# Low parts of weights on VectorE alone, half of the V product's chunks kept in PSUM over all groups, and the weight copies of gathered rows on ScalarE

## The chip, the core and the metric

The kernel runs on one core of one Trainium2 chip. A core has TensorE (PE, matrix products; the loading of a stationary operand is listed apart as PEld), VectorE (DVE), ScalarE (ACT), GpSimd (POOL) and SyncE (SP, which here only issues transfers). Each engine works through its own queue in order. SBUF holds the operands, and TensorE adds up its products in the eight banks of PSUM. The metric is the device time of one execution in microseconds (us).

## The reference, cut to what matters

The reference is a stack of transformer blocks on 512 tokens of width 1024, in float32. The part that the change touches most is the expert layer of the first block. Each token picks 128 of 16,384 experts (8 heads, 16 each) by two rounds of top-16 over products of queries with keys. An expert is one row of a table U and one row of a table V:

```
act = gelu(einsum('td,thkd->thk', x, u_tab[experts])) * gates
y   = einsum('thk,thkd->td', act, v_tab[experts])
```

The inputs are float32 and so is the result. The kernel therefore writes every matrix as a sum of a high and a low part and forms three products, high by high, high by low and low by high.

## The kernel before, in words

*Units and splits.* `weights` (L295) loads one unit of weights, 128 partitions by 1024, into one of the `w_raw` buffers (six in the expert layer). `split` (L284) makes its two parts. ScalarE copies `w_raw` to `w_hi` (L288). Then `w_lo = w_raw - w_hi` (L289) is made on VectorE, or on GpSimd where `eng=nc.gpsimd` is given. There are two buffers of `w_hi` and two of `w_lo`. `product` (L307) then runs 24 matrix instructions on the unit: first the 16 that use `w_hi`, last the 8 that use `w_lo`.

*The expert layer.* For the first 384 tokens ("dense" tokens) all experts are computed and weighted with gates that are mostly zero. For the last 128 tokens only the rows of their own experts are gathered, one token per partition. The layer goes through three stages here called retrieval, scatter and loop.

- Retrieval (`retrieve`): products with `wq`, scores against the keys, and the two rounds of top-16 on VectorE. Between them stand products of the dense tokens with units of U (`reach`, called through `ahead`), whose gelu is put away in DRAM.
- Scatter (`scatter_gates`): for each four tokens VectorE makes two one-hot tiles `hot` (L1216), GpSimd (L1217) and ScalarE (L1221) multiply one of them with the gates, and TensorE multiplies them to the table of gates. More `reach` products stand beside.
- Loop (in `peer`): 16 groups of 8 output chunks `m`. For each chunk VectorE multiplies a gelu tile with its gates (`f`, L949), it is split to `ga` (L288, L289), one unit of V is loaded and split, and one product of 24 instructions goes to a PSUM tile `mm`. VectorE then adds that to the running sum `h` (L984).

*The gathered rows.* `Own.go` (L1043) copies the number of a row to a tile `f` (or `gel`) on VectorE (L1053), and GpSimd issues an indirect transfer of that row of U or V to `own_row` (L1058). A row fetched earlier is used by `Own.use` (L1023): its weight is copied to the same tile `f` on VectorE (L1034), and one instruction of 128x1024 on VectorE multiplies it in (L1037 for U, L1041 for V). The copies tie the rows to the pace of the other work.

*Who makes the low part.* In retrieval, in scatter, in parts of the first block and in the `w_ab` products of the second block the low part is GpSimd's by argument. In the loop a small planner decides for each unit: `less_loaded` adds up costs (1.13 for a VectorE split, 2.3 for a GpSimd split, 1.2 and 1.04 for a row) and takes the engine that ends first. The order of instructions on each engine is made by a scheduler from its own estimate of times.

*PSUM.* In the expert layer four banks are `mm` and four are `aux`. In the loop only `mm` is used, until the end.

Of the kernel before, what the change touches and what calls it, by code (L numbers as in the profile page):

```python
# [11 lines left out]
F32 = mybir.dt.float32  # L12
# [44 lines left out]
def _pairs(b):  # L57
    """[32 groups, 64 states, 16 channels] -> block diagonal over pairs of groups [128, 16, 32]."""
# [15 lines left out]
def _half_cols(w):  # L74
    """The two members of every rotary pair into two halves of a head."""
# [110 lines left out]
class Ctx:  # L186
    """Pools and constants; tokens are `T` columns in `nb` PSUM banks of `hn` each."""
# [9 lines left out]
    def enter(self, name, side):  # L197
        """A pool that `leave` closes; once h is on the right, the sides are exchanged."""
# [13 lines left out]
    def psum(self, mm, aux):  # L212
        """PSUM as `mm` accumulators of all tokens and `aux` single banks."""
# [5 lines left out]
    def raw_units(self, n):  # L219
        """`n` buffers for units of weights, in an order that all that is loaded there keeps."""  # L220
# [5 lines left out]
    def work(self):  # L226
        """Pools of small tiles and of the tiles of norms."""
# [20 lines left out]
def newton_rsqrt(c, v, n):  # L248
    """1/sqrt(v) of a [128, n] tile, elementwise, to float32 accuracy."""
# [13 lines left out]
def exp_exact(c, out, x, n):  # L263
    """exp of a [128, n] tile to float32 accuracy."""
# [30 lines left out]
def weights(c, src, nk, n, eng=None):  # L295
    """Load one unit of weights and split it: two float32r views [128, nk, n]."""
# [5 lines left out]
    split(c, raw, hi, lo, eng=eng)  # L302
# [15 lines left out]
def token_stats(c, acc, width):  # L318
    """rsqrt(mean + eps) per token from partial sums acc [128, T]: [tokens of a tile, tiles]."""
# [15 lines left out]
def along_tokens(c, col):  # L335
    """A per-token column [128, tiles] as a row on all partitions: PSUM banks of `hn` tokens."""
# [15 lines left out]
def square_sum(c, acc, k, src, eng=None, scale=1.0):  # L352
    """acc += (src * scale) squared (the first chunk starts it)."""
# [9 lines left out]
def token_rows(c, acc, width, name):  # L363
    """rsqrt(mean + eps) as rows on all partitions, in SBUF, and as columns."""
# [4 lines left out]
def column_rows(c, col, name):  # L369
    """A per-token column as rows in SBUF."""  # L370
# [7 lines left out]
class Rows:  # L378
    """The rows of a norm, made when first asked for; uses of them wait until `hold` products are under way."""
# [20 lines left out]
class S5:  # L400
    """Powers of the discretised transition, the input and output weights of chunks of 4 tokens."""
# [74 lines left out]
    def scaled(self, dst, src, by, eng, name):  # L476
        """dst = src * by; parts along the second axis, `by` the real and the imaginary part and the negative of that."""
# [9 lines left out]
    def inputs(self, j):  # L487
        """The input weights of position j in a chunk; position 3 comes first."""
# [9 lines left out]
    def transposes(self):  # L498
        """The input weights as the stationary side of products."""
# [10 lines left out]
    def rotations(self, k):  # L510
        """The rotations of positions 2^k and more, after those before, of a chunk."""
# [11 lines left out]
    def powers(self):  # L523
        """The output weights of the state."""
# [17 lines left out]
    def inside(self, q):  # L542
        """The output weights of the chunk itself, of 4 pairs of groups."""
# [16 lines left out]
def s5_states(c, pool, xs, S, hf):  # L560
    """The states before each chunk, of 8 of the 16 pairs of groups; xs is [(position in chunk, channel), pair, chunk]."""
# [38 lines left out]
def s5_outputs(c, pool, xs, S, hf, h, ys):  # L600
    """ys = gelu of the outputs of these pairs."""
# [21 lines left out]
def mix_layer(c):  # L623
    """Block 1 up to the residual after w_out, which becomes c.h."""
    nc, d = c.nc, c.d
    tt = nc.vector.tensor_tensor
    with c.pool("mix", "right") as pool:
# [3 lines left out]
        with c.pool("s5", "right") as s5p:  # L631
# [3 lines left out]
            with c.pool("s5t", "right") as tmp:  # L635
                S = S5(c, s5p, outer, tmp)
                acc = c.norm("acc")
                for k in range(8):
                    x = pool.tile([128, 512], F32, name="u", bufs=5)
                    nc.sync.dma_start(x, d["xT"][:, k])  # L640
                    if k == 0:
                        w = weights(c, d["w_in"][0], 8, 128, eng=nc.gpsimd)
# [7 lines left out]
                for m in range(4):  # L650
                    ps = c.mm()
                    product(c, ps, [((w[0][:, k], w[1][:, k]), xk[k]) for k in range(8)])
                    if m < 3:
                        w = weights(c, d["w_in"][m + 1], 8, 128, eng=None if m else nc.gpsimd)
# [16 lines left out]
                for what, step in [(o[0], int(o[1])) for o in V_ORDER]:  # L671
                    if what == "v":
# [9 lines left out]
                        else:  # L682
                            w = weights(c, d["w_in"][4], 8, 128, eng=nc.gpsimd)
# [12 lines left out]
            for what, step in [(o[0], int(o[1])) for o in U_ORDER]:  # L696
                if what == "u":
                    ps = c.mm()
                    product(c, ps, [((w[0][:, k], w[1][:, k]), xk[k]) for k in range(8)])
                    if step < 3:  # L700
                        w = weights(c, d["w_in"][5 + step], 8, 128, eng=nc.gpsimd)
# [26 lines left out]
            def half(m, k0, pair):  # L728
                """Half of the product of output chunk m; weights come for two chunks at a time."""
# [60 lines left out]
def sgu_norm(c, vn, mean):  # L790
    """The norm of v [token, head, tile, channel] in place, from its sums over channels."""
# [14 lines left out]
def sgu_weights(c, pool):  # L806
    """The causal weights of the mixing, and what it adds."""
# [14 lines left out]
def sgu_mix(c, gp, u, vn, wb):  # L822
    """u *= causal mixing of the normalised v."""
# [21 lines left out]
PER_CALL = 0.6  # L845
# [6 lines left out]
PER_USE = 1.2  # L852
PER_FETCH = 1.04
W_POOL = 2.3
# [1402 lines left out]
```

## Time and profile before

| | |
|---|---|
| median of three runs | 3222.72 us (3222.37 to 3227.86) |
| span of the profiled execution | 3231.5 us |
| DVE busy | 2449.9 us, 76% |
| PE busy, PEld busy | 2989.7 us, 93%; 2704.9 us, 84% |
| ACT busy, POOL busy | 1269.3 us, 39%; 1261.8 us, 39% |

The profiled execution has its span as its only time. It is 0.3% longer than the median of the runs. The expert layer takes the stretch from 257 to 1657 us: retrieval to 598, scatter to 852, loop to 1657. Busy shares are means over stages with different limits, so each stage has to be read by itself. A wait row names the instruction that waited and the one that ended the wait.

### The profile page before, as it was taken

The page shows a single profiled execution, that of the slowest core. Times are in us where ns is not written, and L with a number is a line of the kernel's source. Part 1 is how long each engine was busy: PE and PEld are TensorE (multiplying, and loading weights), DVE is VectorE, ACT ScalarE, POOL GpSimd, SP SyncE. Part 2 cuts the span into 40 slices and gives each one's busy share as a digit, 9 for nine tenths or more (in the row PEclk, how much of TensorE's full clock was granted, in tenths as well). Part 3 has the DMA queues.
Part 4 walks back from the last instruction along what each step waited for, and adds up shares of the span by engine and source line. Part 5 has one row for each costly group of instructions (what it writes and reads, how often), then busy time and mean ns, then how long its engine had stood idle before and what let it go on. Part 6 is the DMA issues. An engine that isn't in the chain of part 4 may idle for free. (4 is left out here: it accounts for less than half of the span.)

```text
span 3231.5 us, 47250 instructions
## 1 busy us (share of the span) xinstructions
PE 2989.7 (93%) x17801; PEld 2704.9 (84%) x17801; DVE 2449.9 (76%) x4680; ACT 1269.3 (39%) x2170; POOL 1261.8 (39%) x786
## 2 busy tenths in 40 slices
PE   4878997899999999999999999899999999999999
PEld 3667997888999999899997899655999997778887
DVE  9977899999799999999998965664534446665352
ACT  3644332577633333333344433144323324443241
POOL 5335566787577677777754202011000012010000
PEclk8988998999999999999999999788999999999999
DMA  2213355566798899998952220011222221022232
GB/s 100 72 53 108 133 170 183 189 229 243 246 311 301 307 305 317 315 311 303 314 198 83 71 73 9 1 47 36 88 92 92 92 86 46 24 79 92 97 98 91
DMA packets 202888, 485.06 MB, mean 150 GB/s; under 512 B 25676, under 2 KB 95780, under 8 KB 199588
## 3 DMA queue, kind: packets, MB, share of 16 engines
q1 hardware_dynamic: 165796, 347.81, 32.3%
q0 software_dynamic: 36864, 134.23, 12.0%
q8 instruction: 140, 2.29, 0.3%
q14 instruction: 88, 0.72, 0.1%
HBM read 437.42 MB, written 44.55 MB: 149 GB/s over the span
## 5 line engine op out<-in xcount | busy, mean ns | idle before, releaser
L288 ACT ACTIVATE w_hi<-w_raw 128x1024 fp32r<-128x1024 f32 (+1 forms) x498 | 511.4, 1028 | 750.7 <-PE mm L314 627.2
L289 POOL TENSOR_TENSOR w_lo<-w_raw,w_hi 128x1024 fp32r<-128x1024 f32 x201 | 532.8, 2653 | 206.5 <-ACT w_hi L288 112.0
L289 DVE TENSOR_TENSOR w_lo<-w_raw,w_hi 128x1024 fp32r<-128x1024 f32 (+1 forms) x297 | 409.2, 1378 | 138.2 <-ACT w_hi L288 96.5
L314 PE MATMUL mm<-hn,w_hi 128*128 128x384 f32 (+1 forms) x2400 | 486.4, 351 | 1.8 <-DVE hn L289 1.3
L314 PEld LDWEIGHTS mm<-hn,w_hi 128*128 128x128 f32 x2400 | 429.0, 191 | 17.8 <-DVE hn L289 1.6
L314 PE MATMUL mm<-ga,w_hi 128*128 128x384 f32 x2048 | 389.6, 343 | 5.5 <-DVE ga L289 3.7
L314 PEld LDWEIGHTS mm<-ga,w_hi 128*128 128x128 f32 x2048 | 368.9, 193 | 8.0 <-DVE ga L289 5.1
L314 PE MATMUL mm<-xg,w_hi 128*128 128x264 f32 (+1 forms) x1920 | 345.9, 334 | 20.5 <-ACT w_hi L288 8.8
L360 POOL TENSOR_TENSOR acc<-acc,sq 128x512 f32<-128x512 f32 (+1 forms) x55 | 86.1, 1570 | 658.7 <-ACT sq L359 654.4
L314 PEld LDWEIGHTS mm<-xg,w_hi 128*128 128x128 f32 x1920 | 290.0, 191 | 59.2 <-DVE xg L292 12.4
L314 PE MATMUL mm<-hn,w_lo 128*128 128x384 f32 (+1 forms) x1200 | 259.1, 353 | 13.7 <-POOL w_lo L289 6.4
L314 PE MATMUL mm<-hid,w_hi 128*128 128x264 f32 (+1 forms) x1536 | 251.1, 319 | 0.0
L1058 POOL DMA_INDIRECT own_row<-V_rows,f x128 | 204.9, 1601 | 92.2 <-DVE f L1034 52.1
L314 PEld LDWEIGHTS mm<-hid,w_hi 128*128 128x128 f32 x1536 | 223.0, 188 | 20.0
L314 PEld LDWEIGHTS mm<-hn,w_lo 128*128 128x128 f32 x1200 | 214.8, 191 | 25.8 <-DVE w_lo L289 9.3
L314 PE MATMUL mm<-ga,w_lo 128*128 128x384 f32 x1024 | 207.3, 345 | 30.8 <-DVE w_lo L289 20.6
L288 ACT ACTIVATE ga<-f 128x384 fp32r<-128x384 f32 x128 | 67.0, 525 | 378.3 <-DVE f L949 370.9
L314 PEld LDWEIGHTS mm<-ga,w_lo 128*128 128x128 f32 x1024 | 182.5, 192 | 38.9 <-DVE w_lo L289 24.2
L1041 DVE SCALAR_TENSOR_TENSOR own_x<-own_row,f,own_x 128x1024 f32<-128x1024 f32 x123 | 195.6, 1590 | 0.5
L314 PE MATMUL mm<-xg,w_lo 128*128 128x264 f32 (+1 forms) x960 | 173.6, 329 | 0.0
L1058 POOL DMA_INDIRECT own_row<-U_rows,f x87 | 129.1, 1484 | 83.5 <-DVE f L1034 64.5
L314 PEld LDWEIGHTS mm<-xg,w_lo 128*128 128x128 f32 x960 | 144.9, 188 | 17.1
(732 smaller groups left out, 5357.2 us busy)
## 6 DMA issues: line engine op xcount, KB each, us to landing
w_raw<-U SPq DMA_DIRECT2D x128, 512.0 KB
w_raw<-V SPq DMA_DIRECT2D x128, 512.0 KB
w_raw<-w_f SPq DMA_DIRECT2D x128, 512.0 KB
g_all<-stage SPq DMA_DIRECT2D x24, 1024.0 KB
g<-g_all SPq DMA_DIRECT2D x32, 768.0 KB
early<-gel SPq DMA_DIRECT2D x70, 192.0 KB
gel<-early SPq DMA_DIRECT2D x70, 192.0 KB
w_raw<-w_ab SPq DMA_DIRECT2D x22, 512.0 KB
```

What stands on the lines that cost most here:

```text
L288: nc.scalar.activation(hi, src, AF.Copy)
L289: (eng or nc.vector).tensor_tensor(lo, src, hi.bitcast(F32), ALU.subtract)
L314: c.nc.tensor.matmul(ps[:, h, :hn], lhsT=st[a], rhs=mv[b][:, h * hn:(h + 1) * hn], start=first and i == 0, stop=last and i == len(order) - 1)
L360: (eng or nc.gpsimd).tensor_tensor(acc, acc, sq, ALU.add)
L1041: stt(self.acc, r, weight, self.acc, op0=ALU.mult, op1=ALU.add)
L1058: nc.gpsimd.indirect_dma_start(out=r, out_offset=None, in_=self.c.d["U_rows" if i0 < 128 else "V_rows"], in_offset=bass.IndirectOffsetOnAx ...
```

## The change

All low parts are made on VectorE: the argument `eng` and the planner `less_loaded` with its constants are gone. In the loop the products of chunks 0 to 3 (`HELD = 4`) go to four `aux` banks that keep adding up over all 16 groups. These are added to `h` once, in the last group. Chunks 4 to 7 are as before. The copy of a gathered row's weight is a ScalarE instruction. The final transposes of the gathered rows' sum (`add`) use an `mm` bank, as the `aux` banks are taken. The changed file has its comment strings blanked, and its line numbers are 3 to 9 lower from the loop on.

```diff
-def split(c, src, hi, lo, scale=None, eng=None):
+def split(c, src, hi, lo, scale=None):
     if scale is None:
         nc.scalar.activation(hi, src, AF.Copy)
-        (eng or nc.vector).tensor_tensor(lo, src, hi.bitcast(F32), ALU.subtract)
+        nc.vector.tensor_tensor(lo, src, hi.bitcast(F32), ALU.subtract)
...
-            w = weights(c, d["U"][a], 8, 128, eng=eng)
+            w = weights(c, d["U"][a], 8, 128)
...
-        def less_loaded():
-            k = 0 if load[0] + 1.13 <= load[1] + W_POOL else 1
-            load[k] += (1.13, W_POOL)[k]
-            return (nc.vector, nc.gpsimd)[k]
...
+            held = [c.aux()[:, None, :] for _ in range(HELD)]
...
-                    w = weights(c, d["V"][8 * g + m], 8, 128, eng=less_loaded())
-                    ps = c.mm()
-                    product(c, ps, [((w[0][:, k], w[1][:, k]), (ga[0][:, k], ga[1][:, k])) for k in range(8)], n=n)
+                    w = weights(c, d["V"][8 * g + m], 8, 128)
+                    keep = m < HELD
+                    ps = held[m] if keep else c.mm()
+                    product(c, ps, [((w[0][:, k], w[1][:, k]), (ga[0][:, k], ga[1][:, k])) for k in range(8)], n=n,
+                            first=not keep or g == 0, last=not keep or g == 15)
                     if g < 15:
                         pace(1)
-                    tt(c.h[m][:, :n], ps[:, 0, :n], c.h[m][:, :n], ALU.add)
+                    if not keep or g == 15:
+                        tt(c.h[m][:, :n], ps[:, 0, :n], c.h[m][:, :n], ALU.add)
...
         if at is not None:
-            nc.vector.tensor_copy(at, weight)
+            nc.scalar.activation(at, weight, AF.Copy)
             weight = at
...
-            w = weights(c, d["wq"][2 * h + k], 8, 128, eng=nc.gpsimd)
+            w = weights(c, d["wq"][2 * h + k], 8, 128)
...
-    load = lambda m: weights(c, d["w_ab"][m], 8, 128, eng=nc.gpsimd)
+    load = lambda m: weights(c, d["w_ab"][m], 8, 128)
```

The order of VectorE's queue in the loop, in the half where rows of V are used: before, one stretch reads as follows (`own_x` is the sum of the gathered rows, `ga` a low part of the activations, `h<-mm` the addition of a product).

```order
L1041 SCALAR_TENSOR_TENSOR own_x<-own_row,f,own_x 128x1024
L949 TENSOR_TENSOR f<-gel_11585,g 128x384
L1053 COPY f<-own_ids 128x1
L984 TENSOR_TENSOR h<-mm,h 128x384
L1034 COPY f<-own_gate 128x1
L289 TENSOR_TENSOR w_lo<-w_raw,w_hi 128x1024
L1041 SCALAR_TENSOR_TENSOR own_x<-own_row,f,own_x 128x1024
L289 TENSOR_TENSOR ga<-f,ga 128x384
L1041 SCALAR_TENSOR_TENSOR own_x<-own_row,f,own_x 128x1024
L984 TENSOR_TENSOR h<-mm,h 128x384
L289 TENSOR_TENSOR w_lo<-w_raw,w_hi 128x1024
```

Here half of the units' `w_lo` stand on this queue, and the others on GpSimd's. In the changed kernel a stretch of the same half of the loop reads:

```order
L1032 SCALAR_TENSOR_TENSOR own_x<-own_row,f,own_x 128x1024
L1044 COPY f<-own_ids 128x1
L975 TENSOR_TENSOR h<-mm,h 128x384
L289 TENSOR_TENSOR w_lo<-w_raw,w_hi 128x1024
L289 TENSOR_TENSOR ga<-f,ga 128x384
L1032 SCALAR_TENSOR_TENSOR own_x<-own_row,f,own_x 128x1024
L938 TENSOR_TENSOR f<-gel_10968,g 128x384
L975 TENSOR_TENSOR h<-mm,h 128x384
L289 TENSOR_TENSOR w_lo<-w_raw,w_hi 128x1024
L1044 COPY f<-own_ids 128x1
L1032 SCALAR_TENSOR_TENSOR own_x<-own_row,f,own_x 128x1024
```

The copies `f<-own_gate` are gone from the queue, the additions `h<-mm` come for half of the chunks only, and every unit's `w_lo` stands in it.

In retrieval VectorE's queue holds the top-16 instructions (MAX, MAX_INDEX and MATCH_REPLACE, which the profile calls MAX8, FIND_INDEX8 and MATCH_REPLACE8; `s`, `i` and `rep` are what they make for one half of a head). A stretch of it before:

```order
L1094 MAX s_2444<-rep_2551 128x8
L1094 MAX s_2444<-rep_2557 128x8
L1095 MAX_INDEX i_2445<-s_2444,rep_2551 128x8
L1095 MAX_INDEX i_2445<-s_2444,rep_2557 128x8
L1093 MATCH_REPLACE rep_2563<-s_2444,sc 128x128
L1093 MATCH_REPLACE rep_2569<-s_2444,sc 128x128
L1094 MAX s_2444<-rep_2563 128x8
L1094 MAX s_2444<-rep_2569 128x8
L1095 MAX_INDEX i_2445<-s_2444,rep_2563 128x8
L1095 MAX_INDEX i_2445<-s_2444,rep_2569 128x8
```

No split stands in it. The same instructions in the changed kernel:

```order
L1085 MAX s_2444<-rep_2551 128x8
L289 TENSOR_TENSOR w_lo<-w_raw,w_hi 128x1024
L1085 MAX s_2444<-rep_2557 128x8
L1086 MAX_INDEX i_2445<-s_2444,rep_2551 128x8
L1086 MAX_INDEX i_2445<-s_2444,rep_2557 128x8
L1084 MATCH_REPLACE rep_2563<-s_2444,sc 128x128
L1084 MATCH_REPLACE rep_2569<-s_2444,sc 128x128
L1085 MAX s_2444<-rep_2563 128x8
L1085 MAX s_2444<-rep_2569 128x8
L1086 MAX_INDEX i_2445<-s_2444,rep_2563 128x8
L1086 MAX_INDEX i_2445<-s_2444,rep_2569 128x8
```

Splits, which stood on GpSimd's queue, now stand among the top-16 instructions, and the instructions behind a split come after it.

ScalarE's queue in the loop, before:

```order
L288 ACTIVATE ga<-f 128x384
L288 ACTIVATE w_hi<-w_raw 128x1024
L288 ACTIVATE ga<-f 128x384
L288 ACTIVATE w_hi<-w_raw 128x1024
L288 ACTIVATE ga<-f 128x384
L288 ACTIVATE w_hi<-w_raw 128x1024 x2
L897 ACTIVATE gel<-mm 128x384
```

It holds copies to `ga` and `w_hi` and the gelu only. A stretch of it in the changed kernel:

```order
L288 ACTIVATE w_hi<-w_raw 128x1024
L1025 ACTIVATE f<-own_gate 128x1 x2
L288 ACTIVATE w_hi<-w_raw 128x1024
L894 ACTIVATE gel<-mm 128x384
L1025 ACTIVATE f<-own_gate 128x1 x3
L288 ACTIVATE ga<-f 128x384
L288 ACTIVATE w_hi<-w_raw 128x1024
L1025 ACTIVATE f<-own_gate 128x1
L288 ACTIVATE ga<-f 128x384
L288 ACTIVATE w_hi<-w_raw 128x1024
```

The copies `f<-own_gate` of 128x1 now stand between the copies that make the high parts.

## Rows read from the trace of the kernel before

**Rows 1.** The page's part 5, GpSimd's splits of all stages.

```profile
L289 POOL TENSOR_TENSOR w_lo<-w_raw,w_hi 128x1024 fp32r<-128x1024 f32 x201 | 532.8, 2653 | 206.5 <-ACT w_hi L288 112.0
```

**Rows 2.** Stretches: length, PE, PEld, DVE, ACT, POOL busy, clock, DMA, GB/s.

```profile
257.00:480.00 223.00, 212.24 (x1105) 193.02 (x1104) 183.12 (x726) 82.88 (x112) 123.42 (x91) 0.96 0.42 141
480.00:598.00 118.00, 96.88 (x500) 92.72 (x498) 117.48 (x251) 34.29 (x47) 80.89 (x49) 0.90 0.61 188
598.00:852.00 254.00, 232.62 (x1495) 219.20 (x1495) 247.80 (x286) 196.19 (x350) 194.16 (x144) 0.99 0.62 221
852.00:1657.00 805.00, 763.20 (x4234) 749.45 (x4233) 774.63 (x1150) 267.03 (x360) 587.74 (x314) 0.98 0.89 306
```

**Rows 3.** Timeline of the loop (start, us, engine and line), five instructions.

```profile
1303.43 1.21 DVE L289 TENSOR_TENSOR w_lo<-w_raw,w_hi 128x1024 fp32r<-128x1024 f32 x1
...
1306.94 3.92 DVE L289 TENSOR_TENSOR w_lo<-w_raw,w_hi 128x1024 fp32r<-128x1024 f32 x1
1307.37 2.40 POOL L289 TENSOR_TENSOR w_lo<-w_raw,w_hi 128x1024 fp32r<-128x1024 f32 x1
...
1311.57 1.27 DVE L1041 SCALAR_TENSOR_TENSOR own_x<-own_row,f,own_x 128x1024 f32<-128x1024 f32 x1
1311.68 2.45 POOL L1058 DMA_INDIRECT own_row<-V_rows,f  x1 [1.91 <-DVE f L1034]
```

**Rows 4.** VectorE by line, 862:1640 (busy us, mean ns | idle before).

```profile
L1041 DVE SCALAR_TENSOR_TENSOR own_x<-own_row,f,own_x 128x1024 f32<-128x1024 f32 x121 | 193.1, 1596 | 0.5
L289 DVE TENSOR_TENSOR w_lo<-w_raw,w_hi 128x1024 fp32r<-128x1024 f32 x74 | 144.9, 1958 | 2.1 <-ACT w_hi L288 1.5 <-issue 0.4
L949 DVE TENSOR_TENSOR f<-gel,g 128x384 f32<-128x384 f32 x127 | 126.5, 999 | 10.7 <-DMA g<-g_all 5.7 <-ACT gel L897 4.6
...
L289 DVE TENSOR_TENSOR ga<-f,ga 128x384 fp32r<-128x384 f32 x126 | 120.4, 959 | 0.5 <-ACT ga L288 0.5
L984 DVE TENSOR_TENSOR h<-mm,h 128x384 f32<-128x384 f32 x118 | 64.8, 549 | 1.4 <-PE mm L314 1.4
...
L1034 DVE COPY f<-own_gate 128x1 f32<-128x1 f32 x123 | 15.1, 141 | 0.0
L1034 DVE COPY f<-ones 128x1 f32<-128x1 f32 x91 | 11.0, 141 | 0.0
```

**Rows 5.** GpSimd by line, the same stretch.

```profile
L289 POOL TENSOR_TENSOR w_lo<-w_raw,w_hi 128x1024 fp32r<-128x1024 f32 x96 | 247.5, 2580 | 36.1 <-ACT w_hi L288 24.6 <-PE mm L314 10.1
```

**Rows 6.** Waits, 880 to 1640 us (total us, times, longest).

```profile
ACT w_hi L288 <- PE mm L314: 69.7, 45, 3.2
...
PEld mm L314 <- DVE w_lo L289: 28.0, 16, 3.2
...
PEld mm L314 <- POOL w_lo L289: 18.5, 18, 2.1
```

**Rows 7.** VectorE by line in scatter, 598 to 852 us.

```profile
L1216 DVE TENSOR_TENSOR hot<-iota,bt 128x512 f32<-128x512 f32 x96 | 119.9, 1249 | 0.5 <-PE aux L1222 0.5
L1216 DVE TENSOR_TENSOR hot<-iota,at 128x512 f32<-128x512 f32 x96 | 97.5, 1016 | 0.0
```

**Rows 8.** GpSimd by line in scatter.

```profile
L289 POOL TENSOR_TENSOR w_lo<-w_raw,w_hi 128x1024 fp32r<-128x1024 f32 x27 | 81.0, 2998 | 2.9 <-PE mm L314 2.9
```

**Rows 9.** VectorE by line in retrieval, 257 to 598 us.

```profile
L1153 DVE TENSOR_TENSOR hit<-hit,expert 128x1600 f32<-128x1600 f32 x16 | 42.1, 2633 | 0.1
L1037 DVE SCALAR_TENSOR_TENSOR own_row<-own_row,gel,own_x 128x1024 f32<-128x1024 f32 x16 | 41.8, 2620 | 0.0
L1149 DVE TENSOR_TENSOR hit<-posf,iota 128x1600 f32<-128x1600 f32 x16 | 29.0, 1810 | 0.1
...
L1091 DVE MAX8 s<-sc 128x8 f32<-128x128 f32 x64 | 14.9, 279 | 34.2 <-ACT sc L1118 34.2
```

**Rows 10.** GpSimd by line in retrieval.

```profile
L289 POOL TENSOR_TENSOR w_lo<-w_raw,w_hi 128x1024 fp32r<-128x1024 f32 x56 | 144.0, 2575 | 72.9 <-PE mm L314 35.0 <-ACT w_hi L288 22.7 <-ACT sc L1118 14.8
```

**Rows 11.** ScalarE by line, a small instruction.

```profile
L1855 ACT ACTIVATE wa_e<-wa_e 128x4 f32<-128x4 f32 x8 | 1.6, 197 | 1.8 <-DVE wa_e L1854 1.8
```

More of the change, by code (lines that the diff above doesn't have):

```diff
@@ L292, in split, with weights @@
         nc.vector.scalar_tensor_tensor(lo, src, scale, hi.bitcast(F32), op0=ALU.mult, op1=ALU.subtract)
-def weights(c, src, nk, n, eng=None):
+def weights(c, src, nk, n):
     nc = c.nc
@@ L301, in weights @@
     lo = c.wp.tile([128, 1024], F32R, name="w_lo", bufs=2)[:, :nk * n]
-    split(c, raw, hi, lo, eng=eng)
+    split(c, raw, hi, lo)
     return [t.rearrange("p (k n) -> p k n", k=nk) for t in (hi, lo)]
@@ L641, in mix_layer @@
                     if k == 0:
-                        w = weights(c, d["w_in"][0], 8, 128, eng=nc.gpsimd)
+                        w = weights(c, d["w_in"][0], 8, 128)
                     split(c, x, xg[0][:, k], xg[1][:, k], scale=c.vec("g_mix", k))
@@ L653, in mix_layer @@
                     if m < 3:
-                        w = weights(c, d["w_in"][m + 1], 8, 128, eng=None if m else nc.gpsimd)
+                        w = weights(c, d["w_in"][m + 1], 8, 128)
                     else:
@@ L682, in mix_layer @@
                         else:
-                            w = weights(c, d["w_in"][4], 8, 128, eng=nc.gpsimd)
+                            w = weights(c, d["w_in"][4], 8, 128)
                     elif what == "b":
@@ L700, in mix_layer @@
                     if step < 3:
-                        w = weights(c, d["w_in"][5 + step], 8, 128, eng=nc.gpsimd)
+                        w = weights(c, d["w_in"][5 + step], 8, 128)
                     u.append(pool.tile([128, 512], F32, name="u", bufs=5))
@@ L844 @@
 G_ROWS = 28
-PER_CALL = 0.6
+HELD = 4
 GEL = 4
@@ L864, in peer @@
         rows = Own(c, gelp)
-        w_q = [weights(c, d["wq"][k], 8, 128, eng=nc.gpsimd) for k in range(2)]
+        w_q = [weights(c, d["wq"][k], 8, 128) for k in range(2)]
         low = [c.raw(F32R) for _ in range(4)]
@@ L882, in peer @@
             nc.vector.scalar_tensor_tensor(t, c.h[k], c.vec("g_ffn", k), row, op0=ALU.mult, op1=ALU.mult)
-            split(c, t, hn[0][:, k], hn[1][:, k], eng=nc.gpsimd if k % 2 else None)
+            split(c, t, hn[0][:, k], hn[1][:, k])
             rows.take(k, t[:, n:])
@@ L889, in peer, with reach @@
         early = {}
-        def reach(a, eng):
-            w = weights(c, d["U"][a], 8, 128, eng=eng)
+        def reach(a):
+            w = weights(c, d["U"][a], 8, 128)
             ps = c.mm()
@@ L898, in reach, with ahead @@
             return gel
-        def ahead(k, eng):
+        def ahead(k):
             for _ in range(min(k, len(first) - len(early))):
@@ L903, in ahead @@
                 early[s] = dram.tile([128, n], F32, name="early%d" % s)
-                nc.sync.dma_start(early[s], reach(s, eng))
+                nc.sync.dma_start(early[s], reach(s))
         place = lambda: gelp.tile([128, 512], F32, name="gel", bufs=GEL)
-        load = [0.0, 0.0]
-        def less_loaded():
-            k = 0 if load[0] + 1.13 <= load[1] + W_POOL else 1
-            load[k] += (1.13, W_POOL)[k]
-            return (nc.vector, nc.gpsimd)[k]
         with c.pool("sel", "right") as sel:
@@ L925, in beside @@
             def beside(i, n):
-                ahead((i + 1) * rest // n - i * rest // n, nc.gpsimd)
+                ahead((i + 1) * rest // n - i * rest // n)
                 rows.go((i + 1) * G_ROWS // n - i * G_ROWS // n, place)
@@ L930, in peer @@
                 scatter_gates(c, sp, at, bt, gt, g_all, beside)
-        ahead(128, nc.gpsimd)
+        ahead(128)
         with c.pool("ga", "right") as gp:
@@ L942, in prepare @@
                 else:
-                    gel = reach(s, less_loaded())
+                    gel = reach(s)
                 if s % 4 == 0:
@@ L963, in pace @@
                 rows.go(k, place)
-                load[0] += PER_USE * k + PER_CALL
-                load[1] += PER_FETCH * k
+            held = [c.aux()[:, None, :] for _ in range(HELD)]
             ga = pair()
@@ L1068, in add @@
         for q in range(2):
-            ps = c.aux()
+            ps = c.mm()[:, 0]
             for k in range(4):
@@ L1154, in pairs_of @@
             nc.vector.tensor_reduce(e_all[:, t, both].rearrange("p h s -> p (h s)"), hit, axis=AX.X, op=ALU.add)
-            ahead(1, nc.vector if t == 0 else nc.gpsimd)
+            ahead(1)
             go(GO_T)
@@ L1164, in retrieve @@
             keys_of(h2, *now)
-            ahead(2, nc.gpsimd)
+            ahead(2)
         if before:
@@ L1170, in retrieve @@
             keys_of(h2 + 1, *now)
-            ahead(2, nc.gpsimd)
+            ahead(2)
             go(GO_H)
@@ L1320 @@
 class Delta:
+    pass
 def delta_inputs(c, keep, pool, xk, rows):
```

3 lines of the change are left out of this document (removed).

## The prediction, made before the changed kernel had run

> **What bounds the kernel now.** I read the share of the span first, then busy times by stretch, then in each stretch of the expert layer what its instructions cost and what TensorE waited for.
>
> GpSimd makes 201 low parts, 2.65 us each [rows 1]. The stretches show what stands beside them [rows 2]. In retrieval's second part (480 to 598 us) VectorE is busy for 117.5 of 118 us, in scatter for 247.8 of 254, in the loop for 774.6 of 805. In those three the reader is to see VectorE full. In the loop TensorE is nearly full too: weight loads cover 749.5 of 805 us.
>
> VectorE is full partly because it stands still. In the timeline of the loop a `w_lo` on VectorE takes 1.21 us, and one that meets a `w_lo` of 2.40 us on GpSimd takes 3.92 [rows 3]: it was held for 2.71 us, about as long as the other ran. The loop's means say the same of all [rows 4]: 128x384 with both inputs in SBUF takes 999 and 959 ns, while 128x384 with one input from PSUM (`h<-mm`, L984) takes 549. Held time is, with 0.55, 1.21 and 1.27 us as the free durations [rows 3, 4]: 127 x 0.45 = 57 us for `f`, 126 x 0.41 = 52 for `ga`, 74 x 0.75 = 55 for `w_lo`, 121 x 0.33 = 39 for `own_x`, together 203 us of the 774.6.
>
> GpSimd also issues row fetches there. A fetch of 2.45 us ran beside an `own_x` of 1.27 us that was not held [rows 3], so a fetch holds VectorE seldom or briefly. I put 180 of the 203 us down to the splits. The ends are 100 (half, as if fetches held as much) and 203.
>
> **The loop (852 to 1657).** GpSimd's row counts 96 splits in 778 us [rows 5]; I take 98 for the whole stretch. VectorE's time changes as follows. The held time goes: -180. The 98 splits come: 98 x 1.21 = +119. Of 128 additions `h<-mm`, chunks 0 to 3 of 15 groups go: 60 x 0.549 = -33 [rows 4]. The copies of weights go: (123 + 91) x 0.141 = -30 [rows 4]. The sum is 774.6 - 124 = 651 us; with 100 us of held time it is 731, with 203 it is 628. In each case VectorE is below the 749.5 us of TensorE's loads [rows 2], so TensorE is late next. What it can win is its waits for low parts, 28.0 us for those of VectorE and 18.5 for those of GpSimd, 46.5 together [rows 6]. VectorE at 85% of a queue in order will still be late at times, so I leave some 8 of the 46.5: -38 us. The ends are 0 and -50.
>
> The Trainium skill, "Trainium Kernel Development and Optimization", section Performance Expectations, warns that matmul busy time is a bad measure of how full TensorE is and that the busy share of weight loads is a good one. By matmul busy time the loop's room would be 805 - 763.2 = 42 us, by loads 55.5 [rows 2]. The waits of 46.5 us lie between the two.
>
> The copies of weights cost ScalarE 214 x 0.2 = 43 us; the nearest row is a 128x4 instruction at 197 ns [rows 11]. ScalarE is busy for 267 of 805 us [rows 2], so the cost itself is hidden. The wait that it adds is not free. A copy stands in ScalarE's queue behind a `w_hi` copy, which waits for TensorE to release its buffer (69.7 us in 45 waits [rows 6], 1.5 us each). VectorE's `own_x` now waits for that copy, and everything behind `own_x` on VectorE too, the next `w_lo` first. VectorE's spare 98 us (749 - 651) cover those 70 us. Without that cover the wait reappears at TensorE, which is a rival below. Keeping sums in PSUM adds no work on TensorE; of the four chunks' additions those of the last group stay.
>
> **Scatter (598 to 852).** A `hot` tile is 128x512. Between 0.55 us for 384 columns and 1.21 for 1024 [rows 3, 4] a free one takes about 0.68. Then held time is 96 x 0.57 = 55 and 96 x 0.34 = 32 us [rows 7], 87 together, by GpSimd's 27 splits (81.0 us [rows 8]) and by its 96 multiplications of `hot` tiles. I put 55 down to the splits: 2 us for each of 27. VectorE: -55 + 27 x 1.21 (33) - 21 copies x 0.14 (3) = -25. VectorE is the limit there, but TensorE's loads already take 219.2 of 254 us, so I take -18. The ends are 0 and -28.
>
> **Retrieval (257 to 598).** The picture is different, because the top-16 instructions have one input and are not held: MAX8 takes 279 ns on average [rows 9], like a free one. Held are `hit<-hit`, 16 x (2.633 - 1.810) = 13 us with the other `hit` of that size as the free one, and `own_row`, 16 x (2.620 - 1.27) = 22 [rows 9]; with smaller ones I take 45. Against this stand 56 splits [rows 10], 56 x 1.21 = 68. VectorE gets 21 us more (45 to 68 less, 2 for copies). It stood idle for 34.2 us until the scores came [rows 9], and splits fit in there. I take +5; the ends are -5 and +21.
>
> **The rest.** 201 - 98 - 27 - 56 = 20 splits lie in the first block and before the delta rule. Each costs VectorE 1.21 us and gives back up to 2.4. I take -3, between -10 and +8.
>
> **Sum.** -38 - 18 + 5 - 3 = -54 us. The profiled execution took 3231.5 us, so 3177.5; the runs' median is 0.997 of it, so **3169 us**. The best ends together give -50 - 28 - 5 - 10 = -93, or 3130.
>
> **Rivals.**
>
> *A split that waits holds VectorE's queue.* GpSimd's splits waited for 72.9 us in retrieval, for buffers that TensorE had not released and for high parts [rows 10], and GpSimd had nothing urgent behind them. On VectorE the top-16 stands behind. If all of that lands there, retrieval's VectorE has 300.6 + 21 + 73 = 395 us to do in 341 [rows 2]: +53. In the loop the same waits (36.1 us [rows 5]) and ScalarE's keep VectorE late, and nothing is won. +53 - 18 = +35, so 3258 us, slower. It decides from the point where retrieval grows by 21 us with no gain in the loop, or by 59 with the gain forecast. For it: the splits stand among the top-16 instructions. Against it: they stand some ten top-16 instructions apart, which with 0.28 us each [rows 9] and 1.21 for the split is 4 us from split to split, so they don't crowd. Chance 9%.
>
> *The copies on ScalarE keep the loop where it is.* VectorE at the upper figure, 731, plus 70 us of waits makes 801, and the loop stays at 805. Then -18 + 5 - 3 = -16: 3207 us. The held-time row of the fetch speaks against the 731. 10%.
>
> *Transfers hold the loop.* DMA is at 0.89 of its time and 306 GB/s [rows 2]. At 767 us it would need 0.93. If it gives no more than now, 3207 again. No row of the loop shows TensorE waiting for a transfer. 7%.
>
> [...] It raises that chance from 5 to 7%.
>
> *Fetches hold VectorE as much as splits did.* Only 100 us of held time go, VectorE is at 731 in the loop and TensorE waits half as much as now: -20 there, -36 in all, 3187 us. 12%.
>
> **How the numbers follow.** The forecast has 56%, with a range of its own of 3150 to 3190; better than 3150 has 6%. The slower rival 9%, the two at 3207 17%, the one at 3187 12%. About 0.2% (6 us) is what a measurement of this kernel can tell from no change. Slower by that has 9%; of the 17% at 3207 about a quarter may end within 6 us of 3222.7 or so, 5%; faster 86%. The range that leaves out 2 in 10 reaches from 3138 to 3212.
>
> **What would show it.** In the loop `f` and `ga` on VectorE near 550 ns instead of 999 and 959; VectorE at about 650 us; the loop at 767 us with weight loads over 97% of it; scatter at 236. Wrong would be: `f` still near 900 ns (fetches hold VectorE), VectorE's `own_x` waiting for ScalarE's copies by more than 100 us in total, TensorE waiting for `w_lo` as long as before, or retrieval longer than 362 us.

## The result, and the profile after

The changed kernel takes 3119.77 us (median of 4 runs, 3114.91 to 3126.16) against 3222.55 us before (4 runs, 3216.28 to 3227.86). The ratio is 0.9689, with a 95% interval of 0.9669 to 0.9708: 103 us faster, where 54 were forecast and 93 was the best case. The direction was right, the size was not.

The two profiled executions differ by 118.4 us (spans of 3231.5 and 3113.1), since that of before took longer than all four timed runs and that of after is the shortest of its four. The stages have other bounds after, so both kernels are shown with the stages cut at the same events: retrieval from the first `own_row` to the first `hot`, scatter to the first product with `ga`, the loop to the last one, and as a fourth row the end of the delta rule, whose code is the same in both. The columns are those of [rows 2]. Before:

```profile
248.10:598.80 350.70, 318.13 (x1641) 292.86 (x1639) 310.26 (x988) 122.59 (x168) 211.82 (x142) 0.94 0.48 154
598.80:871.70 272.90, 252.21 (x1607) 238.80 (x1608) 255.30 (x294) 204.74 (x365) 198.15 (x145) 0.99 0.65 229
871.70:1682.40 810.70, 767.16 (x4259) 753.22 (x4258) 788.79 (x1164) 273.03 (x365) 597.64 (x319) 0.98 0.88 300
2080.70:2356.90 276.20, 254.78 (x1560) 194.25 (x1559) 162.61 (x388) 106.25 (x220) 17.65 (x13) 0.88 0.17 56
```

After:

```profile
240.00:608.20 368.20, 357.62 (x1921) 334.75 (x1920) 340.66 (x1076) 143.94 (x218) 83.04 (x91) 0.98 0.55 182
608.20:824.30 216.10, 191.17 (x1305) 184.52 (x1303) 195.13 (x253) 185.62 (x343) 121.46 (x108) 0.97 0.62 228
824.30:1583.90 759.60, 757.95 (x4281) 757.18 (x4282) 645.06 (x994) 308.63 (x589) 296.76 (x221) 1.00 0.92 320
1976.20:2242.10 265.90, 242.16 (x1561) 189.97 (x1560) 161.82 (x388) 106.55 (x220) 17.43 (x13) 0.93 0.18 58
```

Retrieval grows by 17.5 us, scatter loses 56.8, the loop 51.1, and the first block before them 8.1 (248.1 to 240.0). Of the rest, 10.3 us are the end of the delta rule. I don't put them down to the change: the code there is the same, and in all profiles its length goes with the granted clock (0.88 and 0.93 here, and 0.84 with 287.7 us and 0.95 with 261.2 us in two of the experiments).

In the loop (845 to 1560 us) VectorE's instructions are at their free length, against [rows 4]:

```profile
L289 DVE TENSOR_TENSOR w_lo<-w_raw,w_hi 128x1024 fp32r<-128x1024 f32 x168 | 204.3, 1217 | 74.0 <-ACT w_hi L288 51.9 <-issue 12.1 <-PE mm L314 9.4
L1032 DVE SCALAR_TENSOR_TENSOR own_x<-own_row,f,own_x 128x1024 f32<-128x1024 f32 x123 | 157.2, 1278 | 0.3
...
L938 DVE TENSOR_TENSOR f<-gel,g 128x384 f32<-128x384 f32 x118 | 65.6, 556 | 20.1 <-DMA own_row<-V_rows,f 12.5 <-issue 3.0 <-DMA own_row<-U_rows,f 2.4
L289 DVE TENSOR_TENSOR ga<-f,ga 128x384 fp32r<-128x384 f32 x118 | 65.0, 553 | 0.0
L975 DVE TENSOR_TENSOR h<-mm,h 128x384 f32<-128x384 f32 x60 | 32.9, 548 | 0.8 <-PE mm L314 0.8
```

And yet GpSimd still issues all its fetches there (same stretch):

```profile
L1049 POOL DMA_INDIRECT own_row<-V_rows,f x128 | 171.9, 1343 | 255.2 <-DVE f L1044 167.0 <-DVE own_x L1032 74.7 <-issue 7.9
L1049 POOL DMA_INDIRECT own_row<-U_rows,f x84 | 111.3, 1325 | 174.7 <-DVE f L1044 149.3 <-DVE own_row L1028 15.6 <-issue 9.8
```

212 fetches of 283 us, and `f` takes 556 ns: here no fetch holds VectorE to a degree that the means show. The trace of the kernel before says it of single instructions. Of its `w_lo`, `own_x`, `own_row`, `f` and `ga` in the stretch of [rows 4], 303 ran beside a fetch and no split, and are not longer than the means above. The 139 that ran beside a split have all of the excess, 208 us. So the 203 us held were the splits'.

In scatter, against [rows 7], the `hot` tiles took 217.4 us and take 163.1:

```profile
L1207 DVE TENSOR_TENSOR hot<-iota,at 128x512 f32<-128x512 f32 x96 | 94.1, 980 | 0.0
L1207 DVE TENSOR_TENSOR hot<-iota,bt 128x512 f32<-128x512 f32 x96 | 69.0, 719 | 4.2 <-PE aux L1213 3.2 <-ACT hot L1212 0.5 <-POOL hot L1208 0.5
```

The first still takes 980 ns. GpSimd's multiplications of `hot` tiles, which stay, may be the reason; no run took them away. In retrieval, against [rows 9 and 10], the long instructions are no longer held, and the splits wait little:

```profile
L289 DVE TENSOR_TENSOR w_lo<-w_raw,w_hi 128x1024 fp32r<-128x1024 f32 x73 | 89.1, 1220 | 9.9 <-PE mm L314 5.2 <-ACT w_hi L288 2.4 <-issue 2.2
L1028 DVE SCALAR_TENSOR_TENSOR own_row<-own_row,gel,own_x 128x1024 f32<-128x1024 f32 x26 | 32.8, 1269 | 0.0
...
L1144 DVE TENSOR_TENSOR hit<-hit,expert 128x1600 f32<-128x1600 f32 x16 | 29.1, 1816 | 0.0
```

### The profile page after: what moved, and what is told of

It reads as the page before. It is cut to its first block, busy times and chain, and to the rows that moved or that the text cites. A ratio compares the mean times of both kernels' runs of the same rounds, so it can differ in the third digit from the quotient of the medians.

```text
span 3113.1 us, 47394 instructions
## 1 busy us (share of the span) xinstructions
PE 2940.2 (94%) x17801; PEld 2685.4 (86%) x17801; DVE 2260.9 (73%) x4573; ACT 1308.0 (42%) x2422; POOL 706.7 (23%) x581
## 5 line engine op out<-in xcount | busy, mean ns | idle before, releaser
L289 DVE TENSOR_TENSOR w_lo<-w_raw,w_hi 128x1024 fp32r<-128x1024 f32 (+1 forms) x498 | 597.4, 1200 | 214.5 <-ACT w_hi L288 144.3
L1049 POOL DMA_INDIRECT own_row<-V_rows,f x128 | 171.9, 1343 | 255.2 <-DVE f L1044 167.0
L314 PE MATMUL aux<-ga,w_hi 128*128 128x384 f32 x1024 | 193.0, 339 | 13.9 <-ACT ga L288 13.9
L314 PEld LDWEIGHTS aux<-ga,w_hi 128*128 128x128 f32 x1024 | 181.9, 188 | 14.1 <-ACT ga L288 14.1
L314 PE MATMUL mm<-ga,w_hi 128*128 128x384 f32 x1024 | 191.3, 338 | 0.0
L314 PEld LDWEIGHTS mm<-ga,w_hi 128*128 128x128 f32 x1024 | 181.3, 188 | 0.0
L1049 POOL DMA_INDIRECT own_row<-U_rows,f x87 | 115.8, 1332 | 200.9 <-DVE f L1044 174.9
L1032 DVE SCALAR_TENSOR_TENSOR own_x<-own_row,f,own_x 128x1024 f32<-128x1024 f32 x123 | 157.2, 1278 | 0.3
L314 PE MATMUL mm<-hid,w_lo 128*128 128x264 f32 (+1 forms) x768 | 130.6, 319 | 0.0
L2190 DVE TENSOR_TENSOR h<-mm,h 128x528 f32<-128x528 f32 (+1 forms) x32 | 22.4, 700 | 144.3 <-PE mm L314 144.3
```

The costliest lines, as they stand in the source:

```text
L289: nc.vector.tensor_tensor(lo, src, hi.bitcast(F32), ALU.subtract)
L314: c.nc.tensor.matmul(ps[:, h, :hn], lhsT=st[a], rhs=mv[b][:, h * hn:(h + 1) * hn], start=first and i == 0, stop=last and i == len(order) - 1)
L1032: stt(self.acc, r, weight, self.acc, op0=ALU.mult, op1=ALU.add)
L1049: nc.gpsimd.indirect_dma_start(out=r, out_offset=None, in_=self.c.d["U_rows" if i0 < 128 else "V_rows"], in_offset=bass.IndirectOffsetOnAx ...
L2190: tt(c.sv(c.h[m]), c.pv(ps), c.sv(c.h[m]), ALU.add)
```

## The experiments

My theory was: the gain is the low parts leaving GpSimd, because a split there holds VectorE; the sums in PSUM and the copies on ScalarE matter only where VectorE is the limit. Rival: those two parts carry a good share. A second question was why the gain was twice the forecast. Ratios are to the kernel before, with 95% intervals; differences in us between two kernels are of their medians.

**1. Splits alone.** The kernel before, with every low part on VectorE (its planner then decides nothing):

```diff
-        (eng or nc.vector).tensor_tensor(lo, src, hi.bitcast(F32), ALU.subtract)
+        nc.vector.tensor_tensor(lo, src, hi.bitcast(F32), ALU.subtract)
```

> The kernel before with one edit: every low part is made on VectorE. Additions to h for all eight chunks and the copies of row weights stay on VectorE. Theory (held time: VectorE stood still beside GpSimd's splits, and that is nearly the whole gain): VectorE in the loop does 60 additions x 0.55 + 214 copies x 0.14 = 63 us more than in the changed kernel (645 us), 708 of 760, still below TensorE, so at most 15 us of the 103 are lost: 3120 to 3135. Rival (the room made by PSUM sums and by the moved copies is what lets TensorE run through): the loop falls back by 25 us or more, 3145 or above.

3121.71 us, 0.9698 [0.967, 0.9725]. That is the whole gain, from one line.

**2. The other two parts.** Sums in PSUM and copies on ScalarE; the splits as before:

```diff
+HELD = 4
...
+            held = [c.aux()[:, None, :] for _ in range(HELD)]
...
-            nc.vector.tensor_copy(at, weight)
+            nc.scalar.activation(at, weight, AF.Copy)
```

> The kernel before with the other two edits alone: chunks 0 to 3 kept in PSUM and the weight copies on ScalarE, with GpSimd's splits and the planner as before. Theory (held time): VectorE loses 63 us of its own work in the loop but is held as before, and retrieval and scatter do not change; the loop gives 10 to 25 us, 3198 to 3212. Rival (room on VectorE is what counted, from wherever it comes): 63 us less on a VectorE that was full give the loop its whole 51 us, about 3170.

3195.6 us, 0.9928 [0.9906, 0.995]: 23 us, a little better than the theory's range and far from the rival's. Its loop shortens from 810.7 to 781.7 us. While VectorE is the limit, 57 us less work on it (788.8 to 731.4 us) buy 29 in these two profiles.

**3 and 4. Each of them taken out of the changed kernel.**

```diff
-HELD = 4
+HELD = 0
```

> The changed kernel with HELD = 0: all chunks are added to h on VectorE in every group. Theory: VectorE in the loop 645 + 33 = 678 us of 760, covered: within 6 us of the changed kernel. Rival (the PSUM sums matter): 15 us or more above it.

3121.81 us, 0.9692 [0.9672, 0.9712].

```diff
-            nc.scalar.activation(at, weight, AF.Copy)
+            nc.vector.tensor_copy(at, weight)
```

> The changed kernel with the copies of row weights back on VectorE. Theory: 30 us more on VectorE in the loop, 675 of 760, covered: within 6 us of the changed kernel, either way. Rival (the copies on ScalarE make VectorE wait, as the prediction feared): faster than the changed kernel by 8 us or more.

3123.7 us, 0.9677 [0.9647, 0.9708]. Neither can be told from the changed kernel. Both save VectorE's time, and VectorE is no longer the limit.

**5 to 7. Splits put back on GpSimd, one stage at a time,** in the changed kernel: by the old planner in the loop, by fixed choice in retrieval (`wq` and the early units of U), and at the edges (18 splits in the first block and before the delta rule).

```diff
+            k = 0 if load[0] + 1.13 <= load[1] + 2.3 else 1
...
+                    w = weights(c, d["V"][8 * g + m], 8, 128, eng=less_loaded())
```

> The changed kernel with the planner back in the loop: about half of the loop's low parts on GpSimd, those of all other stages on VectorE. Theory (each stage pays its own held time): the loop falls back by most of what it won, less what the PSUM sums and copies give (they gave the loop 29 us alone), so 20 to 40 us above the changed kernel, 3140 to 3160, with f and ga on VectorE again near 900 ns. Rival (the gain of a stage hangs on the stages before it): less than 10 us.

3138.91 us, 0.9743 [0.9724, 0.9761]: 19 us lost, just under the range. VectorE's rows, 840 to 1600 us:

```profile
L945 DVE TENSOR_TENSOR f<-gel,g 128x384 f32<-128x384 f32 x118 | 150.0, 1271 | 18.4 <-ACT gel L894 9.2 <-DMA own_row<-V_rows,f 3.4 <-DMA g<-g_all 2.7
L289 DVE TENSOR_TENSOR w_lo<-w_raw,w_hi 128x1024 fp32r<-128x1024 f32 x77 | 136.4, 1771 | 19.8 <-ACT w_hi L288 19.5
```

The held time is back (`f` 1271 ns for 556; `ga`, expected near 900, 799 for 553). The loop takes 783.6 us, as in experiment 2 (781.7), which has the same parts in it: of the 51 us that the loop won, the room made by those parts keeps about half.

```diff
-                nc.sync.dma_start(early[s], reach(s))
+                nc.sync.dma_start(early[s], reach(s, nc.gpsimd))
```

> The changed kernel with the low parts of retrieval and scatter (wq and the early products with U) back on GpSimd. Theory: retrieval and scatter together were 39 us shorter, of which the whole comes from held time (129 us of VectorE given back for 105 us of splits, and idle time): 3150 to 3165. What the prediction assumed for these stages (13 us) is the rival: 3130 to 3138.

3143.43 us, 0.9756 [0.9736, 0.9777]: 24 us lost, between the two expectations. Its retrieval is 342.4 us, 25.8 shorter than in the changed kernel, its scatter 276.4, 60.2 longer: what retrieval wins, scatter loses twice. Of these 34 us the median shows 24; in the profile the loop, whose code is unchanged, is 17.9 us shorter (741.7) and the end of the delta rule 21.8 longer.

```diff
-    load = lambda m: weights(c, d["w_ab"][m], 8, 128)
+    load = lambda m: weights(c, d["w_ab"][m], 8, 128, eng=nc.gpsimd)
```

> The changed kernel with the low parts of the first block (six units of w_in) and of w_ab (twelve) back on GpSimd. The first block was 8 us shorter and the second block 15 us. Theory: the first 8 us and some 5 of the second block are held time, 3128 to 3135. Rival (both are the spread of single executions or of the granted clock): within 4 us of the changed kernel.

3136.63 us, 0.9739 [0.9719, 0.9758]: 17 us lost by 18 splits, more than expected. The losses of 5 to 7 add up to 60 us, not 103, which left 43 us open.

**8 and 9. Work on GpSimd without a use.** To see the hold itself: GpSimd runs, twice for each of 96 units of the loop, an instruction on a weight tile whose result nobody reads. First an addition with two inputs, then a copy with one.

```diff
+                            nc.gpsimd.tensor_tensor(c.norm("sq", 2), c.last_raw[:, :512], c.last_raw[:, 512:], ALU.add)
```

> The changed kernel with useless work on GpSimd in the loop: for 96 of the 128 units of V it adds the two halves of w_raw (two inputs of 128x512, twice per unit, some 1.2 us each), to a tile that nobody reads; VectorE still makes every low part. It takes nothing from VectorE's or TensorE's work. Theory (GpSimd's instruction holds VectorE): f and ga near 900 ns again, 150 to 230 us more held time on VectorE, so VectorE at 800 to 870 us in the loop and the loop 40 to 110 us longer. Rival (GpSimd's splits cost by being late for TensorE, 2.4 us instead of 1.2): f and ga stay near 555 ns and the loop stays within 5 us of 760.

3269.16 us (one run), loop 894.3 us, 135 more and beyond the range; `f` and `ga` at 725 and 754 ns, below the 900 expected. VectorE's rows from 860 to 1700 us, then GpSimd's:

```profile
L289 DVE TENSOR_TENSOR w_lo<-w_raw,w_hi 128x1024 fp32r<-128x1024 f32 x166 | 274.5, 1662 | 3.9 <-ACT w_hi L288 2.9 <-issue 1.0
...
L289 DVE TENSOR_TENSOR ga<-f,ga 128x384 fp32r<-128x384 f32 x118 | 88.9, 754 | 0.6 <-ACT ga L288 0.5
```
```profile
L971 POOL TENSOR_TENSOR sq<-w_raw 128x512 f32<-128x512 f32 x174 | 285.9, 1665 | 79.0 <-DMA w_raw<-V 77.9
```

A stretch of its timeline shows one meeting:

```profile
1302.93 2.51 POOL L971 TENSOR_TENSOR sq<-w_raw 128x512 f32<-128x512 f32 x2
...
1303.15 3.39 DVE L1036 SCALAR_TENSOR_TENSOR own_x<-own_row,f,own_x 128x1024 f32<-128x1024 f32 x1
...
1306.93 1.27 DVE L1036 SCALAR_TENSOR_TENSOR own_x<-own_row,f,own_x 128x1024 f32<-128x1024 f32 x1
```

The first `own_x` ends 3.39 us after its start, that is 1.10 us after GpSimd's pair, a little under its own free length. Over the loop the excess of `w_lo`, `own_x`, `own_row`, `ga` and `f` over the changed kernel's means is 165 us, 0.95 us for each of 174 additions of 1.67. It reaches TensorE: its loads wait 96 us for low parts from VectorE (84.8 for `w_lo`, 11.5 for `ga`), where in the changed kernel they wait 0.9. The size of the growth isn't clean: fetches stand in GpSimd's queue behind additions that wait for a weight tile (77.9 us), and VectorE waits for rows. Hence the next run.

```diff
+                            nc.gpsimd.tensor_copy(c.norm("sq", 2), c.last_raw[:, :512])
```

> As beside_two, but GpSimd's useless work has one input: it copies the first half of w_raw (128x512), twice per unit, for the same 96 units. It waits for the same transfers and stands in front of the same row fetches as in beside_two. Theory that GpSimd's instruction holds VectorE whatever its number of inputs: f, ga and w_lo on VectorE longer in proportion to GpSimd's time, the loop 20 us or more over 760. Rival (it holds VectorE only while it reads two tiles, or the row fetches queued behind it made beside_two slow): f and ga near 555 ns; the loop then shows what the queue of fetches alone costs.

3142.96 us (one run), loop 771.3 us, 12 more. VectorE in its loop (840 to 1590 us), then GpSimd:

```profile
L289 DVE TENSOR_TENSOR w_lo<-w_raw,w_hi 128x1024 fp32r<-128x1024 f32 x174 | 226.4, 1304 | 12.1 <-ACT w_hi L288 6.8 <-issue 2.6 <-PE mm L315 2.3
...
L289 DVE TENSOR_TENSOR ga<-f,ga 128x384 fp32r<-128x384 f32 x120 | 79.3, 662 | 4.1 <-ACT ga L288 4.1
```
```profile
L971 POOL COPY sq<-w_raw 128x512 f32<-128x512 f32 x177 | 185.4, 1070 | 63.1 <-DMA w_raw<-V 62.7
```

The same excess is 58 us, 0.33 us for each copy of a mean of 1.07. The means hide how alike the two runs are, since GpSimd's instructions are longer too where they meet VectorE's. Shortest, median and longest of copies and of additions (ns):

```profile
L971 POOL COPY sq<-w_raw x177: 600/931/1997, 844.8 to 1589.0; 128x512 f32<-128x512 f32 x177
L971 POOL TENSOR_TENSOR sq<-w_raw x174: 1257/1580/2497, 868.7 to 1697.4; 128x512 f32<-128x512 f32 x174
```

A copy by itself takes 0.60 us, an addition 1.26. The instructions on VectorE that were held by a copy were so for 0.40 us (median), those held by an addition for 1.08: in both runs some 0.2 us less than GpSimd's instruction takes by itself. So an instruction with one input holds VectorE as one with two does, for less time because it is shorter. The copies wait for the tile nearly as long (62.7 us), with the same fetches behind them, so that queue costs 12 us at most here. In the run before, VectorE's work in the loop (818.6 us) was 61 us more than TensorE's loads take without waits (757.2); what the rest of the 135 us is made of stays open, and each of the two runs is a single one.

**10 and 11. Earlier products with U.** If VectorE's room in retrieval draws products forward, more of them may be asked for: 80 or 84 units of U ahead of the loop instead of 70.

```diff
-EARLY = 70
+EARLY = 80
```

> The changed kernel with EARLY = 80 instead of 70: ten more products with U are made in retrieval and scatter, where TensorE stood idle for 35 us (368 - 358 and 216 - 191 us busy), and ten fewer in the loop, where it was full. Theory (the loop is now TensorE's and the two stages before it VectorE's): the loop 10 x 4.2 = 42 us shorter, the stages before it longer by 10 x 1.2 us of splits and a few more, so 15 to 28 us faster than the changed kernel, 3092 to 3105. Rival (transfers of 320 GB/s or VectorE bound the loop as well): less than 8 us.

3100.25 us, 0.9636 [0.9612, 0.9659], within the range.

```diff
-EARLY = 70
+EARLY = 84
```

> The changed kernel with EARLY = 84. Theory: fourteen more products need 59 us of TensorE before the loop, more than the 35 us in which it stood idle there, so the gain over EARLY = 80 is under 6 us. Rival (the stages before the loop wait for VectorE alone): 10 to 14 us faster than EARLY = 80.

3103.14 us, 0.9649 [0.9629, 0.967]: no more than at 80.

**12. The last of GpSimd's arithmetic.** The additions of squares, 128x512 with two inputs, go to VectorE:

```diff
-        (eng or nc.gpsimd).tensor_tensor(acc, acc, sq, ALU.add)
+        (eng or nc.vector).tensor_tensor(acc, acc, sq, ALU.add)
```

> The changed kernel with the additions of squares (L360, 55 on GpSimd at 1.58 us) on VectorE. Theory (each held VectorE for about as long as it would take VectorE, 0.68 us, and stood in the chain that starts a layer): 4 to 12 us faster, 3108 to 3116. Rival (VectorE is not the limit where they stand, so neither held time nor their own time counts): within 4 us.

3108.29 us, 0.9659 [0.9636, 0.9683]: 11 us better, as expected. Which of the theory's two reasons it is, held time or the chain, this run doesn't separate.

**13 to 15. The open 43 us.** The same stages the other way round: in the kernel before, only one stage's splits go to VectorE. If held time overlaps across stages, these don't add up either; if the putting back was cheap because the other two parts had made room, they do.

```diff
-            return (nc.vector, nc.gpsimd)[k]
+            return nc.vector
```

> The kernel before with the loop's low parts on VectorE and all others as before; nothing kept in PSUM, copies on VectorE. Theory (each stage pays its own held time, and the parts add up): the loop 811 to 755 us, 3220 - 56 = 3160 to 3170. Rival (the parts need each other, as the three single removals added up to 60 us of 103 only): 3185 or above.

3163.72 us, 0.9827 [0.9795, 0.9858].

```diff
-                nc.sync.dma_start(early[s], reach(s, eng))
+                nc.sync.dma_start(early[s], reach(s, nc.vector))
```

> The kernel before with the low parts of retrieval and scatter alone on VectorE. Theory (adding up): those stages 30 to 40 us shorter, 3180 to 3190. Rival (as when they were put back in the changed kernel): 3194 to 3200.

3187.31 us, 0.9898 [0.9865, 0.993].

```diff
-    load = lambda m: weights(c, d["w_ab"][m], 8, 128, eng=nc.gpsimd)
+    load = lambda m: weights(c, d["w_ab"][m], 8, 128)
```

> The kernel before with the six units of w_in and the twelve of w_ab alone on VectorE. Theory: 6 us in the first block and 7 in the second, 3203 to 3211. Rival (the 17 us of edges_pool were the spread of its second block's later part): within 5 us of before.

3207.53 us, 0.996 [0.9941, 0.9979]. All three are within the theory's ranges. The gains are 0.0173 + 0.0102 + 0.0040 = 0.0315, and the whole change gave 0.0311: 56, 33 and 13 us. They add up, within intervals of together some 15 us to either side. So the 43 us are mostly the room of the other two parts: of the loop's 56 us experiment 5 lost only 19, and those parts give the loop 29 by themselves (experiment 2). The stages of the run with the splits of retrieval and scatter alone show where the 33 come from:

```profile
248.30:618.50 370.20, 359.64 (x1929) 336.82 (x1928) 339.27 (x1096) 142.31 (x193) 87.49 (x95) 0.98 0.55 181
618.50:843.70 225.20, 198.89 (x1322) 191.45 (x1321) 204.93 (x274) 187.54 (x342) 123.64 (x110) 0.95 0.62 224
843.70:1642.30 798.60, 761.58 (x4258) 750.00 (x4257) 767.40 (x1159) 271.54 (x363) 583.82 (x319) 0.99 0.88 303
```

**16. Both gains together:** the edits of 10 and 12 in the changed kernel.

> The changed kernel with EARLY = 80 and the additions of squares on VectorE. Theory: the two work in different stages and add up: 3084 to 3094. Rival (they share the same slack): 3097 to 3101.

3063.88 us (6 runs, 3058.2 to 3068.28), 0.9515 [0.9491, 0.9539]: 56 us better than the changed kernel, 20 beyond the range's better end. It beats both. Its stages:

```profile
233.40:589.00 355.60, 346.30 (x1872) 325.03 (x1871) 330.05 (x1062) 140.18 (x209) 65.41 (x81) 0.98 0.54 179
589.00:825.50 236.50, 232.61 (x1595) 230.02 (x1593) 213.80 (x279) 199.80 (x372) 127.18 (x113) 1.00 0.71 251
825.50:1538.60 713.10, 705.52 (x4041) 700.91 (x4042) 642.32 (x981) 291.58 (x569) 298.10 (x221) 1.00 0.96 338
```

Scatter, which after the change left TensorE without loads for 31.6 of 216.1 us, now has loads for 230.0 of 236.5, and the loop has 240 loads fewer. In the profile of experiment 10 these are nearly the same (229.9 of 236.6, 4042 loads in the loop). Why the two edits give more together than 20 and 11 us is not settled. Of the 40 us between the two profiles, 15 lie at the end of the delta rule, at a granted clock of 0.88 and 0.93, and all six runs here were granted more (0.967 to 0.970 on average) than the four of experiment 10 (0.959 to 0.961).

## Why the prediction was right in direction and half the size

**Right: what bounds, and why.** VectorE was full because GpSimd's splits held it. Splits alone give the whole gain (experiment 1), and in the loop VectorE came to 645 us where 651 was forecast. That the two are so near is in part luck: in the same cut VectorE's time fell by 143.7 us (788.8 to 645.1), not by 124, because the 180 us of held time put down to the splits should have been 203.

The Trainium skill, "SBUF — State Buffer", section SBUF: two separate sides, says that a VectorE instruction with two SBUF inputs and a GpSimd instruction that reads SBUF share a port pair under a lock: whichever starts first has it for the whole instruction, and the other is blocked. The traces agree on the block, for two-input work (`own_x` 3.39 us instead of 1.27) and for one-input copies (held for 0.40 us by copies of 0.60). They don't show that the first to start has it: the `w_lo` of 3.92 us began 0.43 us before GpSimd's [rows 3] and was held.

**Too small: the loop, -38.** By the single-stage run it was worth 56 us. The step was right that TensorE is late next, but it counted only the 46.5 us of waits for low parts of weights [rows 6] and left 8 of them. All of TensorE's idle time went: 810.7 - 753.2 = 57.5 us without loads before, 759.6 - 757.2 = 2.4 after. Beside the waits for `w_lo`, TensorE's loads had waited 5.1 us for VectorE's `ga` and 3.6 for ScalarE's copies, and no low part came late any more (0.9 us). In the profiles the loop is 51.1 us shorter and not 55 because it has 24 loads more (4258 to 4282).

**The step that failed: scatter, -18, "TensorE's loads already take 219.2 of 254 us".** I took the loads as a floor. They were movable work: products with U, which may stand in retrieval, in scatter or in the loop. TensorE's weight loads in scatter by line, before and then after:

```profile
L314 PEld LDWEIGHTS mm<-hn,w_hi 128*128 128x128 f32 x559 | 96.3, 189 | 0.1
L314 PEld LDWEIGHTS mm<-hn,w_lo 128*128 128x128 f32 x280 | 48.7, 189 | 0.0
```
```profile
L314 PEld LDWEIGHTS mm<-hn,w_hi 128*128 128x128 f32 x352 | 60.7, 188 | 0.0
L314 PEld LDWEIGHTS mm<-hn,w_lo 128*128 128x128 f32 x183 | 32.1, 188 | 0.0
```

304 loads of 188 ns, 57 us, left scatter, and scatter is 56.8 us shorter. Most of them moved into retrieval (1639 to 1920 loads), where TensorE had stood without loads for 57.8 us, and 24 into the loop. Retrieval grew by 17.5 us, where +5 had been taken. Retrieval and scatter together gave 39.3 us in the profiles and 33 in the single-stage run; the forecast was +5 - 18 = -13.

The loads did not move because VectorE ran faster: their place in TensorE's queue changed. In the kernel before, 2465 loads stand ahead of the first load of a `hot` tile; in the changed kernel 2777 do, which is 13 units of U more. The scheduler sets this order from its own estimates, and it goes with the engine of these splits: 2444 or 2465 loads in every run that leaves retrieval's splits to GpSimd (experiments 2, 6, 13 and 15), 2718 to 2777 in every run that has them on VectorE. No run changes the engine and keeps the order. So the floor failed, but how much of the 33 to 39 us is held time and how much is the new order stays open. In the loop the order changed too, but there experiment 8 brought held time back with the splits on VectorE.

**Under-sized: the held time of both stages, 55 + 45 = 100 us.** VectorE's time in them fell by 29.8 us (565.6 to 535.8) although its low parts rose from 17.4 to 122.1 and only 5 us of copies left: 129 us of held time went. The `hot` tiles gave 54 of the 55 foreseen. `hit<-hit` (13) and `own_row` (27) gave a little more than the 35 foreseen of them. What was missed are some 35 in many smaller instructions, where 10 had been put. One kind of these has a single input: the 16 casts `posf<-pos` of retrieval took 719 ns each before and 174 after.

**Under-sized: the rest, -3.** It was 13 us (experiment 15): 18 splits, 0.7 us each.

Against the forecast these make 18 (loop), 20 (retrieval and scatter) and 10 (rest): 48 of the 49 us missed. That it comes out to 1 us is luck, with intervals of 6 to 11 us to either side of the three gains.

**The rivals.** The wait in VectorE's queue did not come: its splits waited for 9.9 us in retrieval, not 73. The copies on ScalarE did not hold the loop (waits in it after, 824.3 to 1583.9 us):

```profile
ACT w_hi L288 <- PE mm L314: 137.9, 69, 3.2
...
DVE w_lo L289 <- ACT w_hi L288: 52.6, 37, 2.9
```

ScalarE's wait for buffers doubled against [rows 6], and VectorE waits behind it, but VectorE has 114 us to spare. Transfers gave 320 GB/s where 306 had been read, and 338 in experiment 16, without a wait of TensorE. VectorE's 98 added splits did not make the fetches later, and no run shows a reason to raise this chance from 5 to 7%: a fetch of a row of V took 1601 ns on average before and 1343 after. That fetches hold VectorE is refuted by `f` at 556 ns.

## What to carry to other kernels

Before giving arithmetic to GpSimd, look at what runs on VectorE at that time: if it has two inputs in SBUF, compare a meeting in the timeline with a free instruction of the same shape, and charge GpSimd's work with what VectorE loses. When work is taken from one engine, don't take another engine's busy time in the next stage for a floor: ask which of that work may stand elsewhere, and compare the order of the queues before and after, since a scheduler that plans by engine moves other work along with the edit. And savings on an engine that another edit takes off the limit are worth nothing (experiments 3 and 4), though alone they were worth 23 us.

## What was not expected of the hardware

- GpSimd's copy with one input of 128x512 (0.60 us by itself) held VectorE's instructions for 0.40 us, its addition with two inputs (1.26 us) for 1.08. Per GpSimd instruction, met or not, that was 0.33 and 0.95 us. 212 indirect fetches beside VectorE held it for nothing that its means show.
- The loop without idle TensorE isn't of one length: 4257 loads took 741.3 us in experiment 13, 4282 took 757.2 in the changed kernel, both at a granted clock of 1.00. Why a load takes 174 ns in the one and 177 in the other is open.
- The end of the delta rule, the same code in every kernel, took from 261 us at a granted clock of 0.95 to 288 at 0.84. Differences of under 15 us between two profiles have to be looked up stage by stage before they are put down to an edit.
